# Second feed-forward entry: 1/z by ScalarE, squares added by DMAs, two more weights split in attention

## The chip, the cores and the metric

One core of a Trainium2 chip runs the whole program. The metric is the device time of one execution in microseconds (us), lower is better. The engines that matter here are TensorE (PE, matrix products), VectorE (DVE, elementwise), ScalarE (ACT, functions from tables, copies), GpSimd (POOL, which here issues transfers and reduces over partitions) and SyncE (SP, which only issues transfers). Each engine runs its own instructions in the order in which they were written and waits at an instruction until its inputs are there and its buffer is free.

## What is computed

Two layers of a decoder on a sequence of 1024 positions with 1024 channels: a short gated convolution, a dilated attention of three branches, and behind each of them a SwiGLU feed-forward network of 2816 hidden channels. Cut to what the change touches:

```
def rms_norm(x, g):
    y = xf * lax.rsqrt(jnp.mean(xf * xf, axis=-1, keepdims=True) + EPS)
    return (y * g).astype(x.dtype)

def dilated_attention_mixer(h, w_qkv, w_out, rel_bias):
    ...
    alpha = jax.nn.softmax(jnp.stack(lses, axis=0), axis=0)
    o = jnp.sum(alpha[..., None] * jnp.stack(outs, axis=0), axis=0)
    return o.reshape(bsz, seq, D_MODEL).astype(h.dtype) @ w_out

def reference(x, ...):
    for i in range(DEPTH):
        h = rms_norm(x, mix_norm[i])
        x = x + (short_conv_mixer(...) if i % 2 == 0 else dilated_attention_mixer(...))
        h = rms_norm(x, ffn_norm[i])
        x = x + swiglu(h, ffn_w_gate[i], ffn_w_up[i], ffn_w_down[i])
    return rms_norm(x, final_norm)
```

In the kernel the three branches of attention share one sum: `o` holds the unnormalised output of a pair of heads and `z` its denominators, so that the output is o times 1/z.

## The kernel before

Activations lie transposed: eight tiles X[0] to X[7] of 128 channels by 1024 positions, each worked on in two halves of 512 positions. Every float32 operand is split into a high and a low part of the type fp32r (`split`, L138 on ScalarE copies the high part, L139 on VectorE subtracts for the low part), and a product is three matmuls: high by high, high by low, low by high. Weights come from HBM through pages called `raw` (SP's queue, L152), are split, and stand in a list `ops` in the order of use; `ensure(n)` splits ahead up to place n of that list.

The place of the change is the end of attention and the entry into the second feed-forward network.

- **The last slot of attention.** The output product of attention has two groups: group 0 takes five of the eight head pairs, group 1 (`("ao", 1, n)`, weights of 128x384) takes pairs 5, 6 and 7. Group 0 runs inside the last slots as filling for TensorE. Just before the last slot, `ensure(ahead_ao)` splits the weights of group 1 for the first five tiles (`AO_WIDE` = 5).
- **`finish(p)`, last pair.** z and o are copied out of PSUM by ScalarE (L1486, L1487). For earlier pairs 1/z takes a way through DRAM. For the last pair VectorE takes the reciprocal of 128x256 pieces in place (L1518), multiplies o (L1512), and after each half o is split into `o_hi` and `o_lo`.
- **Group 1 (`by_columns`).** It runs the eight tiles of X for the first half and then for the second half, nine matmuls each (L347 to L349). The first three tiles of the first half run abreast. Behind each tile VectorE adds the product to X (L466), ScalarE squares the tile for the norm (`Norm.chained`) and sends it to a spill buffer (L1220), and some weights of the feed-forward network are split.
- **`Norm.chained`, the sum of squares.** In the second entry `by_dma` is false: the square of tile 0 goes to `acc` (L427), each later one to a buffer `sq` (L420) that VectorE adds to `acc` one tile later (L422). In the first entry `by_dma` is true: tile 1's square goes to a second buffer `acc2` (called `odd`); the squares of tiles 2 and 4 are added to `acc`, those of 3 and 5 to `acc2`, by transfers that accumulate, issued by POOL (L429); VectorE adds tile 6's square, `acc2` and tile 7's square (L430).
- **The statistics.** `stats` sums `acc` over channels on TensorE (L445), takes the root on ScalarE (L448) and the reciprocal on VectorE (L449), and spreads 1/rms over partitions by a diagonal matrix (L454) and a matmul (L461); ScalarE copies it to `rstd` (L462). For the first half this stands among the tiles of the second half. From then on VectorE makes the operands of the first half, `hcol` (L1063) and its low part (L526), between the additions to X. For the second half L445 stands behind the first two products of the feed-forward network (L533 to L535), and `second_half` (L1093) needs its `rstd`.
- `gained` (L1085, and L1089 by POOL's accumulating transfers) prepares the second half's operands.

PSUM has eight banks of 128x512, given out in turn; a bank is free again when the addition or copy that reads it is done. Nothing but the order in the code places the work.

Of the kernel before, what the change touches and what calls it, by code (L numbers as in the profile page):

```python
# [12 lines left out]
AF = mybir.ActivationFunctionType  # L13
ALU = mybir.AluOpType
# [3 lines left out]
S = 1024  # L18
# [5 lines left out]
HALF = 512  # L24
# [21 lines left out]
AO_WIDE = 5  # L46
# [48 lines left out]
def trunk(ctx: ExitStack, tc: tile.TileContext, x, gains_in, cwi, ck, cwo, wqkv, wo, relb,  # L95
          wg, wu, wd, oneh, ident, out):
    nc = tc.nc
# [6 lines left out]
    def page(name, dt=F32):  # L104
        return pages.tile([128, 1024], dt, name=name, tag="page", bufs=PAGES)
# [3 lines left out]
    def half_page(name, dt=F32):  # L109
        return scope["pool"].tile([128, 512], dt, name=name, tag="half", bufs=scope["halves"])  # L110
# [4 lines left out]
    def half(h):  # L115
        return slice(h * HALF, (h + 1) * HALF)
# [11 lines left out]
    def split(src, dst=None, eng=nc.vector):  # L128

        w = src.shape[1]  # L130
        if dst is None:
            if w <= HALF:
                t = page("w", F32R)
                dst = t[:, :w], t[:, HALF:HALF + w]
            else:
                dst = page("w_hi", F32R)[:, :w], page("w_lo", F32R)[:, :w]
        hi, lo = dst
        nc.scalar.activation(hi, src, AF.Copy)  # L138
        eng.tensor_tensor(out=lo, in0=src, in1=hi, op=ALU.subtract)  # L139
        return hi, lo  # L140
# [4 lines left out]
    ops, made, op_state = [], {}, [0, 0]  # L145
    combos, raw_base, sums_of = {}, {}, {}

    def load_raw(upto):
        while raw_state[0] < min(upto + 1, len(raw_src)):
            i = raw_state[0]  # L150
            raw_tile[i] = page("raw")
            nc.sync.dma_start(raw_tile[i][:, :raw_src[i].shape[1]], raw_src[i])  # L152
            raw_state[0] += 1
# [5 lines left out]
    def ensure(upto):  # L159
        while op_state[0] < min(upto + 1, len(ops)):  # L160
            key = ops[op_state[0] + 1][0] if op_state[0] + 1 < len(ops) else None
            if key in sums_of:
                sums_of.pop(key)()
            made[op_state[0]] = ops[op_state[0]][1]()
            op_state[0] += 1
# [186 lines left out]
    def run(*gens):  # L352
        for _ in zip(*gens):
            pass
        for g in gens:
            for _ in g:
                pass
# [12 lines left out]
    X = [None] * KT  # L370

    class Norm:
        def __init__(self, gi):
            self.g = gi
            self.h = {}
            self.acc = self.rstd = None
            self.put_off = None
            self.by_dma = True

        def flush(self):  # L380

# [22 lines left out]
        def add(self, k):  # L404

            hi, lo = page("h_hi", F32R), page("h_lo", F32R)
            nc.scalar.activation(hi, X[k], AF.Identity, scale=self.gain(k))
            nc.vector.scalar_tensor_tensor(lo, X[k], self.gain(k), hi, op0=ALU.mult, op1=ALU.subtract)
            self.h[k] = (hi, lo)
            self.square(k)  # L410

        def chained(self, k, c0, c1):

            s = slice(c0, c1)
            if self.acc is None:
                self.acc, self.rstd = page("acc"), page("rstd")
            acc = self.acc[:, s]
            if not self.by_dma and k:
                to = half_page("sq")
                nc.scalar.activation(to, X[k][:, s], AF.Square)  # L420
                self.flush()
                self.put_off = lambda: nc.vector.tensor_tensor(out=acc, in0=acc, in1=to, op=ALU.add)  # L422
                return
            if k == 1:
                self.odd = half_page("acc2")
            to = half_page("sq") if k > 1 else self.odd if k else acc
            nc.scalar.activation(to, X[k][:, s], AF.Square)  # L427
            if 1 < k < 6:
                nc.gpsimd.dma_start(out=(acc, self.odd)[k % 2], in_=to, accum_op=ALU.add)  # L429
            add = lambda t: nc.vector.tensor_tensor(out=acc, in0=acc, in1=t, op=ALU.add)  # L430
            if k == KT - 1:
                self.flush()
                add(self.odd)
                self.odd = None
            if k > 5:
                self.put_off = lambda: add(to)
# [615 lines left out]
    class Swiglu(Strassen):  # L1052
# [6 lines left out]
        def scaled(self, n, h, t, x=None):  # L1059

            rstd = self.norm.rstd[:, half(h)]
            if x is None:
                nc.vector.scalar_tensor_tensor(t, X[n][:, half(h)], self.norm.gain(n), rstd, op0=ALU.mult, op1=ALU.mult)  # L1063
            else:
                nc.vector.tensor_tensor(out=t, in0=x, in1=rstd, op=ALU.mult)
            return t
# [129 lines left out]
    def into_ffn(i, norm):  # L1196

        sw = Swiglu(i, norm)
        norm.by_dma = not i
        begin = i  # L1200

        pre = []
        first_op = [k for k, f in ops].index(("m", (i, 0), 1))

        def step(k):
            next(pre[0], None)
            sw.gained(k)

        def group1(key, ks, acts):
            def added(j, n):  # L1210

                if j == 0 and n > 3:
                    if n + 2 < KT:
                        ensure(op_state[1] + 1)
                    ensure(first_op + n - 4)
                elif j and n < 2:
                    ensure(first_op + n + 4)

            def between(j, n):
                nc.scalar.dma_start(spill[n][:, half(j)], X[n][:, half(j)])  # L1220
                if j == 0:
                    if n == 3:
                        load_raw(raw_base[i] + 3)
                        if not i:
                            nc.scalar.activation(less, gains, AF.Copy, scale=-1.0)
                    elif n == KT - 1:
                        norm.flush()
                        if i:
                            nc.scalar.activation(scratch, eps, AF.Sqrt)
                elif n == begin:  # L1230
                    pre.append(norm.stats(0, HALF))
                    next(pre[0])
                    for m in (6, 7):
                        combos[i, 0](m)
                elif n > begin:
                    if n == begin + 1:
                        run(pre.pop())
                        pre.append(sw.first_half())
                    plan = ((0, 1), (2,), (3,), (4,), (5,), (6, 7)) if i else ((0,), (1,), (2, 3), (4,), (5,), (6,), (7,))
                    for k in plan[n - begin - 1]:  # L1240
                        step(k)

            by_columns((key, 1), ks, acts, HALVES, lambda n, c: norm.chained(n, *c), between,
                       3 if key == "ao" else 4, added=added)

        def last_step():
            run(pre[0])
            norm.flush()

        return sw, group1, norm.stats(HALF, S), last_step  # L1250
# [19 lines left out]
    def attention(norm):  # L1270
# [11 lines left out]
        parts = {}  # L1282
# [207 lines left out]
        def finish(p):  # L1490

            o, z = OZ.pop(p)
            if p < NPAIR - 1:
                zd, rd = zdram[p]
                nc.sync.dma_start(zd, z[0:65:64])
                yield
                zc = scope["pool"].tile([128, 16], F32, name="zc", tag="zc", bufs=2)
                nc.sync.dma_start(zc, bass.AP(zd.tensor, zd.offset, [[16, 128], [1, 16]]))
                yield
                nc.vector.reciprocal(zc, zc)  # L1500
                nc.sync.dma_start(bass.AP(rd.tensor, rd.offset, [[16, 128], [1, 16]]), zc)
                yield
                nc.sync.dma_start(z, bass.AP(rd.tensor, rd.offset, [[S, 2], [0, 64], [1, S]]))
                yield
                put_off.append((p, o, z))
                return

            acts[p] = page("o_hi", F32R), page("o_lo", F32R)

            def scaled(c0, c1):  # L1510
                q = slice(c0, c1)
                nc.vector.tensor_tensor(out=o[:, q], in0=o[:, q], in1=z[:, q], op=ALU.mult)  # L1512

            def parts(h):
                split(o[:, half(h)], [t[:, half(h)] for t in acts[p]])

            for c in range(0, S, 256):
                nc.vector.reciprocal(z[:, c:c + 256], z[:, c:c + 256])  # L1518
                scaled(c, c + 256)
                if c % HALF:  # L1520
                    parts(c // HALF)
                yield

        def attended():
# [96 lines left out]
            next(later, None)  # L1621
        run(later)
        live = {}
        ahead_ao = [k for k, f in ops].index(("ao", 1, AO_WIDE - 1))
        for p in range(NPAIR):
            last = p == NPAIR - 1
            if p < NPAIR - 2:
# [58 lines left out]
    with tc.tile_pool(name="first", bufs=1) as scope["pool"]:  # L1686
# [4 lines left out]
        norm = Norm(1)  # L1691
# [11 lines left out]
    with tc.tile_pool(name="third", bufs=1) as scope["pool"]:  # L1703
# [3 lines left out]
        norm = Norm(4)  # L1707
# [135 lines left out]
```

## Time and profile before

| What | us |
|---|---|
| median of 3 runs | 2198.8 (2198.76 to 2199.12) |
| time of the profiled execution | 2194.63 |
| its span, first to last instruction | 2192.6 |
| mean granted clock of TensorE | 0.992 |
| ScalarE busy | 999.8 |
| GpSimd busy | 161.9 |

In the profile's rows a group or an instruction reads: line, engine, operation, output<-input by the program's names, shape, count; then busy time and the mean in ns of one, and the engine's idle time ahead with what ended it. In rows in order of time the start and the duration stand in front. An arrow in square brackets names the engine and tile that an instruction had waited for. Rows of stretches give the busy time and count of each engine, then the granted clock, the busy share of the transfer engines and GB/s.

### The profile page before, as it was taken

The page shows a single profiled execution, that of the slowest core. Times are in us where ns is not written, and L with a number is a line of the kernel's source. Part 1 is how long each engine was busy: PE and PEld are TensorE (multiplying, and loading weights), DVE is VectorE, ACT ScalarE, POOL GpSimd, SP SyncE. Part 2 cuts the span into 40 slices and gives each one's busy share as a digit, 9 for nine tenths or more (in the row PEclk, how much of TensorE's full clock was granted, in tenths as well). Part 3 has the DMA queues.
Part 4 walks back from the last instruction along what each step waited for, and adds up shares of the span by engine and source line. Part 5 has one row for each costly group of instructions (what it writes and reads, how often), then busy time and mean ns, then how long its engine had stood idle before and what let it go on. Part 6 is the DMA issues. An engine that isn't in the chain of part 4 may idle for free.

```text
span 2192.6 us, 30554 instructions
## 1 busy us (share of the span) xinstructions
PE 2133.3 (97%) x11138; PEld 1821.9 (83%) x11138; DVE 1759.4 (80%) x3239; ACT 999.8 (46%) x1812; POOL 161.9 (7%) x212
## 2 busy tenths in 40 slices
PE   7899999999999999999999999999999999999998
PEld 6788888778888878878999999887778888888887
DVE  7797848988888798965677777769988888889886
ACT  6433426444443444434455555525544444454435
POOL 0000001010101000010111111110000101000000
PEclk9999999999999999999999999999999999999999
DMA  4122543222323374423333333544223333365432
GB/s 155 54 83 75 204 156 92 97 92 97 120 97 120 93 280 144 132 82 132 91 91 91 91 91 84 170 124 165 71 77 106 108 103 107 100 234 194 159 91 78
DMA packets 133568, 259.50 MB, mean 118 GB/s; under 512 B 47642, under 2 KB 58922, under 8 KB 133418
## 3 DMA queue, kind: packets, MB, share of 16 engines
q1 hardware_dynamic: 75978, 184.80, 26.1%
q0 software_dynamic: 16272, 49.65, 6.4%
q10 hardware_dynamic: 41168, 23.10, 3.5%
q8 instruction: 88, 1.44, 0.3%
q14 instruction: 62, 0.51, 0.1%
HBM read 187.04 MB, written 66.26 MB: 116 GB/s over the span
## 4 chain that ended last, share of the span: by engine, by line
PE 78%; DVE 13%; ACT 4%; DMA 3%; issue 2%; ACTq 0%; SPq 0%; DVEq 0%
PE bank L533 15%; PE bank L535 15%; PE bank L534 15%; PE bank L349 5%; PE bank L347 5%; PE bank L348 5%; PE bank L1463 4%; PE bank L625 3%; PE bank L627 3%; PE bank L628 3%; DVE w L139 2%; DVE b L526 1%; DVE combo L186 1%; PE bank L1391 1%; PE bank L1390 1%
## 5 line engine op out<-in xcount | busy, mean ns | idle before, releaser
L533 PE MATMUL bank<-b,w 128*128 128x512 f32 x1784 | 704.6, 395 | 25.7 <-DVE part L543 6.4
L535 PE MATMUL bank<-b,w 128*128 128x512 f32 x1784 | 700.7, 393 | 8.7 <-DVE w L139 8.7
L534 PE MATMUL bank<-b,w 128*128 128x512 f32 x1784 | 701.2, 393 | 0.0
L533 PEld LDWEIGHTS bank<-b,w 128*128 128x128 f32 x1784 | 338.8, 190 | 102.1 <-ACT part L539 7.5
L535 PEld LDWEIGHTS bank<-b,w 128*128 128x128 f32 x1784 | 338.7, 190 | 84.1 <-DVE w L139 12.7
L534 PEld LDWEIGHTS bank<-b,w 128*128 128x128 f32 x1784 | 338.5, 190 | 69.7 <-issue 0.7
L138 ACT ACTIVATE w<-combo 128x512 fp32r<-128x512 f32 (+2 forms) x464 | 234.5, 534 | 281.2 <-DVE combo L186 275.2
L139 DVE TENSOR_TENSOR w<-combo,w 128x512 fp32r<-128x512 f32 (+2 forms) x464 | 260.2, 574 | 57.6 <-ACT w L138 56.0
L539 ACT ACTIVATE part<-bank 128x512 f32<-128x512 f32 x168 | 99.5, 593 | 270.2 <-PE bank L535 265.1
L139 DVE TENSOR_TENSOR w<-raw,w 128x512 fp32r<-128x512 f32 (+2 forms) x316 | 169.1, 559 | 17.2 <-ACT w L138 15.6
L543 DVE TENSOR_TENSOR part<-part,bank 128x256 f32<-128x256 f32 (+1 forms) x348 | 158.5, 485 | 26.5 <-PE bank L535 14.3
L138 ACT ACTIVATE w<-raw 128x512 fp32r<-128x512 f32 (+2 forms) x316 | 150.6, 519 | 46.4 <-PE bank L535 11.2
L754 DVE TENSOR_TENSOR x<-x,bank 128x512 f32<-128x512 f32 x168 | 114.2, 680 | 31.1 <-PE bank L535 31.0
L347 PE MATMUL bank<-w_hi,w 128*128 128x512 f32 (+1 forms) x320 | 119.8, 374 | 2.6 <-ACT w L138 2.6
L349 PE MATMUL bank<-w_hi,w 128*128 128x512 f32 (+1 forms) x320 | 118.1, 369 | 0.7 <-DVE w L139 0.7
L348 PE MATMUL bank<-w_lo,w 128*128 128x512 f32 (+1 forms) x320 | 117.8, 368 | 0.0
L466 DVE TENSOR_TENSOR x<-x,bank 128x512 f32<-128x512 f32 (+1 forms) x104 | 66.0, 641 | 60.5 <-PE bank L349 52.2
L186 DVE TENSOR_TENSOR combo<-raw 128x512 f32<-128x512 f32 (+1 forms) x160 | 102.9, 643 | 3.8 <-DMA raw<-in_conv_w_in 3.8
L347 PE MATMUL bank<-h_hi,w_hi 128*128 128x512 f32 x256 | 104.6, 409 | 0.0
L349 PE MATMUL bank<-h_hi,w_lo 128*128 128x512 f32 x256 | 100.2, 391 | 0.7 <-DVE w_lo L139 0.7
L348 PE MATMUL bank<-h_lo,w_hi 128*128 128x512 f32 x256 | 99.9, 390 | 0.0
L1137 ACT ACTIVATE part<-part 128x512 f32<-128x512 f32 x66 | 39.7, 628 | 109.7 <-DVE part L543 109.7
(249 smaller groups left out, 3835.2 us busy)
## 6 DMA issues: line engine op xcount, KB each, us to landing
hin<-part SPq DMA_DIRECT2D x126, 256.0 KB
raw<-in_ffn_w_gate SPq DMA_DIRECT2D x44, 512.0 KB
raw<-in_ffn_w_up SPq DMA_DIRECT2D x44, 512.0 KB
part<-sum POOLq DMA_DIRECT2D x72, 256.0 KB, 2.7
raw<-in_ffn_w_down SPq DMA_DIRECT2D x48, 384.0 KB
x<-spill SPq DMA_DIRECT2D x24, 512.0 KB
raw<-in_attn_w_qkv SPq DMA_DIRECT2D x24, 512.0 KB
raw<-in_conv_w_in SPq DMA_DIRECT2D x21, 512.0 KB
```

Source lines behind the costliest of these rows:

```text
L138: nc.scalar.activation(hi, src, AF.Copy)
L139: eng.tensor_tensor(out=lo, in0=src, in1=hi, op=ALU.subtract)
L186: eng.tensor_tensor(out=c, in0=a, in1=b, op=op)
L347: nc.tensor.matmul(b, whi[:, a], ahi[:, s], start=first, stop=False)
L348: nc.tensor.matmul(b, whi[:, a], alo[:, s], start=False, stop=False)
L349: nc.tensor.matmul(b, wlo[:, a], ahi[:, s], start=False, stop=last)
L533: nc.tensor.matmul(b, hi[:, a], bhi, start=start and k == 0, stop=False, skip_group_check=True)
L534: nc.tensor.matmul(b, hi[:, a], blo, start=False, stop=False, skip_group_check=True)
L535: nc.tensor.matmul(b, lo[:, a], bhi, start=False, stop=k == n - 1, skip_group_check=True)
L539: nc.scalar.activation(t, b, AF.Copy)
L543: nc.vector.tensor_tensor(out=t, in0=t, in1=b, op=ALU.add)
L754: nc.vector.tensor_tensor(out=X[n][:, half(h)], in0=X[n][:, half(h)], in1=b, op=ALU.add)
```

## The change

Three edits.

1. For the last pair, 1/z is exp(-ln z): ScalarE takes Ln of the whole z (128x1024) and then, by halves, Exp with scale -1; VectorE multiplies a half of o at a time. The reciprocals are gone.
2. `by_dma` is gone: the second entry adds the squares of tiles 2 to 5 by transfers, as the first does.
3. `ahead_ao` reaches two weights further: seven of group 1's eight weights are split before the last slot.

```diff
-            self.by_dma = True
...
-            if not self.by_dma and k:
-                to = half_page("sq")
-                nc.scalar.activation(to, X[k][:, s], AF.Square)
-                self.flush()
-                self.put_off = lambda: nc.vector.tensor_tensor(out=acc, in0=acc, in1=to, op=ALU.add)
-                return
...
-        norm.by_dma = not i
...
-            for c in range(0, S, 256):
-                nc.vector.reciprocal(z[:, c:c + 256], z[:, c:c + 256])
-                scaled(c, c + 256)
-                if c % HALF:
-                    parts(c // HALF)
+            nc.scalar.activation(z, z, AF.Ln)
+            for h in range(2):
+                nc.scalar.activation(z[:, half(h)], z[:, half(h)], AF.Exp, scale=-1.0)
+                scaled(h * HALF, h * HALF + HALF)
+                parts(h)
                 yield
...
-        ahead_ao = [k for k, f in ops].index(("ao", 1, AO_WIDE - 1))
+        ahead_ao = [k for k, f in ops].index(("ao", 1, AO_WIDE + 1))
```

Line numbers of the changed kernel are 7 or 8 lower than those of the kernel before (L466 is L459, L422 is gone, L430 is L423, L526 is L519, L1063 is L1056).

How the order moves, first on ScalarE at the end of the last slot, from the splits of group 1's weights to the first square. Before:

```order
L138 ACTIVATE w<-raw 128x384 x5
L1486 ACTIVATE z<-bank 64x512
L1487 ACTIVATE o<-bank 64x512
L1486 ACTIVATE z<-bank 64x512
L1487 ACTIVATE o<-bank 64x512
L138 ACTIVATE o_hi<-o 128x512 x2
L427 ACTIVATE acc<-x 128x512
```

And with the change:

```order
L138 ACTIVATE w<-raw 128x384 x7
L1478 ACTIVATE z<-bank 64x512
L1479 ACTIVATE o<-bank 64x512
L1478 ACTIVATE z<-bank 64x512
L1479 ACTIVATE o<-bank 64x512
L1509 ACT_TABLE_LOAD
L1509 ACTIVATE z<-z 128x1024
L1511 ACT_TABLE_LOAD
L1511 ACTIVATE z<-z 128x512
L138 ACTIVATE o_hi<-o 128x512
L1511 ACTIVATE z<-z 128x512
L138 ACTIVATE o_hi<-o 128x512
```

Two splits stand ahead of the copies of z, and two table loads, one Ln and two Exp between the copies and `o_hi`.

On VectorE, the end of the second half's stretch, from the addition to tile 6 of X to the last addition of squares. Before:

```order
L466 TENSOR_TENSOR x<-x,bank 128x512
L422 TENSOR_TENSOR acc<-acc,sq 128x512
L1063 SCALAR_TENSOR_TENSOR hcol<-x,gains,rstd 128x512
L526 TENSOR_TENSOR b<-hcol,b 128x512
L466 TENSOR_TENSOR x<-x,bank 128x512
L422 TENSOR_TENSOR acc<-acc,sq 128x512
L1063 SCALAR_TENSOR_TENSOR hcol<-x,gains,rstd 128x512
L526 TENSOR_TENSOR b<-hcol,b 128x512
L1063 SCALAR_TENSOR_TENSOR hcol<-x,gains,rstd 128x512
L526 TENSOR_TENSOR b<-hcol,b 128x512 x2
L422 TENSOR_TENSOR acc<-acc,sq 128x512
```

And with the change:

```order
L459 TENSOR_TENSOR x<-x,bank 128x512
L1056 SCALAR_TENSOR_TENSOR hcol<-x,gains,rstd 128x512
L519 TENSOR_TENSOR b<-hcol,b 128x512
L459 TENSOR_TENSOR x<-x,bank 128x512
L423 TENSOR_TENSOR acc<-acc,sq 128x512
L423 TENSOR_TENSOR acc<-acc,acc_13620 128x512
L1056 SCALAR_TENSOR_TENSOR hcol<-x,gains,rstd 128x512
L519 TENSOR_TENSOR b<-hcol,b 128x512
L1056 SCALAR_TENSOR_TENSOR hcol<-x,gains,rstd 128x512
L519 TENSOR_TENSOR b<-hcol,b 128x512 x2
L423 TENSOR_TENSOR acc<-acc,sq 128x512
```

The additions of squares between the tiles are gone; behind tile 7 stand those of tile 6's square, of the second buffer (`acc_13620`, the `acc2` of the code) and, last as before, of tile 7's square.

On POOL, from the last transfer of attention to the second half's transfers (L1082 is L1089 before). Before, the four `x<-x` followed the first row at once; with the change:

```order
L1521 DMA odram_91<-o 128x1024
L422 DMA acc<-sq 128x512
L422 DMA acc_13482<-sq 128x512
L422 DMA acc<-sq 128x512
L422 DMA acc_13482<-sq 128x512
L422 DMA acc<-sq 128x512
L422 DMA acc_13620<-sq 128x512
L422 DMA acc<-sq 128x512
L422 DMA acc_13620<-sq 128x512
L1082 DMA x<-x 128x512 x4
```

Eight accumulating transfers have come in, four for each half, two and two into one buffer.

## The prediction

> **What bounds the kernel now.** I read the page's first part, then the waits of TensorE and its order of time around the entry into the second feed-forward network, then what VectorE and ScalarE do there.
>
> ```profile
> span 2192.6 us, 30554 instructions
> PE 2133.3 (97%) x11138; PEld 1821.9 (83%) x11138; DVE 1759.4 (80%) x3239; ACT 999.8 (46%) x1812; POOL 161.9 (7%) x212
> ```
>
> TensorE sets the time: only its waits can be won. The profiled execution took 2194.63 us (span 2192.6); the median of the runs is 2198.8, 4.2 above. The sums below are made in the span, and I take their difference off the median. The waits of TensorE from 1483 to 1600 us, where all three edits lie (total, times, longest):
>
> ```profile
> PE bank L445 <- DVE acc L422: 4.0, 1, 4.0
> PE bank L535 <- DVE w L139: 2.3, 2, 1.9
> PE bank L347 <- ACT w L138: 1.6, 1, 1.6
> ```
>
> In order of time, with the last matmul before each wait and the first ones after it:
>
> ```profile
> 1500.60 0.39 PE L349 MATMUL bank<-o_hi,w 128*128 128x512 f32 x1
> 1502.57 0.50 PE L347 MATMUL bank<-w_hi,w 128*128 128x512 f32 x1 [1.58 <-ACT w L138]
> ...
> 1532.75 0.39 PE L535 MATMUL bank<-b,w 128*128 128x512 f32 x1
> 1537.16 1.05 PE L445 MATMUL bank<-ones,acc 128*128 128x1 f32 x8 [4.02 <-DVE acc L422]
> 1538.07 0.60 PE L533 MATMUL bank<-b,w 128*128 128x512 f32 x1
> ...
> 1541.81 0.39 PE L533 MATMUL bank<-b,w 128*128 128x512 f32 x1
> ```
>
> At full clock a matmul of 512 columns starts every 0.23 us. **Loss A**: 1502.57 - 1500.60 - 0.23 = 1.74 us, for the sixth output weight. **Loss B**: 1537.16 - 1532.75 - 0.23 = 4.18 us, for the sum of squares of the second half. **Loss C**: behind B the nine matmuls from 1538.07 take 3.74 us where 9 x 0.23 = 2.07 would do: 1.7 us, at half clock. Together 7.6 us, the most that this change can win. The 2.3 us at L535 lie after the second statistics, and no edit touches them.
>
> Why VectorE is late, by its groups from 1485 to 1538:
>
> ```profile
> L466 DVE TENSOR_TENSOR x<-x,bank 128x512 f32<-128x512 f32 x19 | 12.7, 679 | 0.0
> L422 DVE TENSOR_TENSOR acc<-acc,sq 128x512 f32<-128x512 f32 x14 | 9.6, 685 | 0.3
> L1518 DVE RECIPROCAL z<-z 128x256 f32<-128x256 f32 x4 | 7.0, 1745 | 0.0
> ```
>
> Its idle time there is about 3 us of 53: it runs behind TensorE throughout, and the four reciprocals put it there. Neighbours overlap, so that an addition of 128x512 costs 0.60 us from start to start.
>
> **The change part by part.** *Two more weights split in attention.* Tile 5 of the product finds its weight; tile 6 likewise, and tile 7's is split after tile 3's square, some 4 us before use. Loss A goes: -1.74. The price is two splits ahead of the copies of z on ScalarE.
>
> *1/z by ScalarE.* VectorE loses 7.0 us of reciprocals; its four multiplications become two of twice the width. ScalarE gains two table loads, Ln and two Exp; their prices, and the landing of a weight from SP's queue:
>
> ```profile
> 1481.31 2.16 ACT L138 ACTIVATE w<-raw 128x384 fp32r<-128x384 f32 x5
> 1485.33 0.59 ACT L1487 ACTIVATE o<-bank 64x512 f32<-64x512 f32 x1
> 1510.08 0.64 ACT L420 ACTIVATE sq<-x 128x512 f32<-128x512 f32 x1 [0.65 <-DVE x L466]
> 1510.73 1.28 ACT L1229 ACT_TABLE_LOAD   x1
> L1453 ACT ACTIVATE lf<-lf 128x1024 f32<-128x1024 f32 x16 | 16.9, 1056 | 45.1 <-DMA vx<-vdram 24.2 <-DVE lf L1452 20.8
> ...
> 1481.97 0.33 SPq L152 DMA_DIRECT2D raw<-in_attn_w_out  x1
> 1494.93 0.39 PE L348 MATMUL bank<-o_lo,w 128*128 128x512 f32 x1
> ...
> 1459.97 0.32 SPq L1607 DMA_DIRECT2D x<-spill  x1
> 1462.73 0.69 DVE L466 TENSOR_TENSOR x<-x,bank 128x512 f32<-128x512 f32 x1 [7.85 <-DMA x<-spill]
> 1475.77 0.32 SPq L1597 DMA_DIRECT2D oin<-odram  x1
> 1480.35 1.06 ACT L138 ACTIVATE w_hi<-oin 128x1024 fp32r<-128x1024 f32 x1 [0.95 <-DMA oin<-odram]
> ```
>
> The seventh weight is issued at 1481.97. Two loads of this queue took 2.8 and 4.6 us until their reader ran; I take 2.8, the emptier queue: split 1484.8 to 1485.2, four copies to 1487.7 (1485.9 before). Then 1.28 + 1.06 (Exp's row for Ln) + 1.28 + 0.63 = 4.25: 1491.9. Multiplication, o_hi, o_lo at some 0.7 each: 1494.0. TensorE wants o_lo at 1494.93: 0.9 to spare, so it costs nothing; the cover is the two other tiles of the product ahead. With 4.6 us it would be 0.9 late, and all behind it too. VectorE waits meanwhile with two additions to tile 7 of x behind it; their banks come back five tiles later. From 1499 it has caught up with TensorE.
>
> *Squares by DMA.* Of seven additions per half three stay. Where the first half's sum ends, VectorE is no longer late. The stretch that sets B:
>
> ```profile
> 1513.39 0.68 DVE L466 TENSOR_TENSOR x<-x,bank 128x512 f32<-128x512 f32 x1
> ...
> 1518.12 0.68 DVE L466 TENSOR_TENSOR x<-x,bank 128x512 f32<-128x512 f32 x1
> 1519.99 1.41 DVE L1063 SCALAR_TENSOR_TENSOR hcol<-x,gains,rstd 128x512 f32<-128x512 f32 x2 [1.19 <-ACT rstd L462]
> ...
> 1522.05 0.68 DVE L466 TENSOR_TENSOR x<-x,bank 128x512 f32<-128x512 f32 x1
> 1522.64 0.69 DVE L422 TENSOR_TENSOR acc<-acc,sq 128x512 f32<-128x512 f32 x1
> 1523.24 0.74 DVE L1063 SCALAR_TENSOR_TENSOR hcol<-x,gains,rstd 128x512 f32<-128x512 f32 x1
> ...
> 1536.42 0.68 DVE L422 TENSOR_TENSOR acc<-acc,sq 128x512 f32<-128x512 f32 x1
> ```
>
> The addition at 1513.39 (tile 1, second half) now follows its bank, which A's end brings to 1511.5; its square, r and diag (0.6 to 1.0 us each) reach 1514.1, three combos 1516.0, tile 2's addition and square 1517.3, rstd 1517.9. So hcol starts at 1517.9, not 1519.99: 2.1 us earlier. From there to TensorE's L445 it was 17.17 us of queued VectorE work; five additions of squares leave it and two come in: 17.17 - 3 x 0.60 = 15.4. The sum is ready for TensorE at 1533.3; I add 0.1 for a landing (below): 1533.4 against 1537.16, a gain of **3.7**. TensorE comes there at 1532.98 - 1.74 = 1531.2, so a wait of 2.2 stays in place of 4.18: A's 1.74 + 2.0 is the same 3.7. All behind, rstd and the second half's operands, moves with it.
>
> The eight DMAs run as in the first entry. L1089's four stand behind them on POOL, an engine that is 7% busy:
>
> ```profile
> PE bank L445 <- DVE acc L430: 0.8, 1, 0.8
> ...
> DMA to landing us min/median/max: 3.2/3.2/4.2
> ...
> DMA to landing us min/median/max: 3.2/3.4/5.1
> ```
>
> These are TensorE's wait for the sums there, the landing of its eight accumulating DMAs, and of the eight of L1089 (same size, same queue, four of them in this entry). Tiles 3 and 5 add into one buffer, one after the other; tile 5's square ends at 1525.0, and VectorE wants the sum at 1528.7: 3.7 us. At 3.2 no wait, at 4.2 one of 0.5, at 5.1 of 1.4; 0.1 taken.
>
> **Loss C** depends on the clock. Two other waits and the granted clock (last column but two) in the 3 us behind these and behind A:
>
> ```profile
> 71.56 0.47 PE L533 MATMUL bank<-b,w 128*128 128x512 f32 x1 [2.17 <-DVE part L543]
> 71.60:74.60 3.00, 3.00 (x13) 2.38 (x14) 2.79 (x5) 1.90 (x4) 0.00 (x0) 1.00 0.39 85
> 1640.43 0.60 PE L533 MATMUL bank<-b,w 128*128 128x512 f32 x1 [2.25 <-ACT part L539]
> 1640.50:1643.50 3.00, 3.00 (x8) 2.35 (x9) 2.31 (x7) 1.71 (x6) 0.00 (x0) 0.53 0.00 0
> 1502.60:1505.60 3.00, 3.00 (x13) 2.30 (x14) 3.00 (x6) 2.31 (x5) 0.00 (x0) 1.00 1.02 301
> ```
>
> A wait of 1.58 leaves the clock whole; 2.25 halves it, 2.17 does not. A wait of 2.2 may go either way; I let the half clock stay, so C gives nothing. The Trainium skill (TensorE: Matmul & The Clock Gate, "HAM oscillation — how this bites in real kernels") says that gaps over about 3.4 us throttle; by it C would go, as in the first rival, but the wait of 2.25 speaks against it.
>
> Sum: 2198.8 - 3.7 = **2195.1 us**. Its own range: rstd 0.5 earlier or 0.3 later, landings up to 5.1: gain 2.2 to 4.4, 2194.4 to 2196.6.
>
> **Rivals.** *The half clock goes too.* The 2.2 us of wait do not halve the clock: gain 3.7 + 1.7 = 5.4, 2193.4. For it the row at 71.56, against it that at 1640.43.
>
> *Wait B goes wholly.* If VectorE gets 2.2 us ahead of my sum, all 7.6 us are won: 2191.2. For it the first entry, where the second half's sum costs TensorE nothing; against it that a tile of this product has 9 matmuls, 2.1 us, in which VectorE has 1.9 us of its own.
>
> *1/z comes late.* Table loads or the seventh weight take longer than my rows, o_lo passes 1494.93, and every us beyond is lost on TensorE: 0.9 late by the 4.6 us landing, 2196.0. Against it: the row at 1510.73 starts 0.01 us after the square before it ends, with no pause. The Trainium skill (ScalarE: Activation LUTs, "What ACT_TABLE_LOAD costs") adds a drain of 1.38 us to each switch; two would make o_lo 1.9 late, 2197.0 by an estimate from that page; the trace's row shows none.
>
> *The accumulating DMAs are the new wait: slower.* VectorE stands in order at the sum of the two buffers, and rstd, hcol and all operands behind it. Tile 3's DMA starts at 1521.4 and tile 5's cannot start before it lands: ready at 1521.4 + 2 landings. Above 3.7 us each further us costs two; at 5.5 the whole gain is gone, at 7.7 the kernel is 4.4 slower: 2203.2. For it: 5.1 us among L1089's landings, with spills and weight loads in the same 16 engines; against it the first entry's 4.2 at most.
>
> **How the numbers follow.** Forecast 0.43, half clock gone 0.25, wait gone 0.10, 1/z late 0.12, DMAs late 0.10. 0.2% is 4.4 us, about what a measurement tells from none. Faster by more: the first two rivals and a fifth of the forecast, 0.44. Slower by more: most of the last, 0.08. Within: 0.48. The range reaches from the whole 7.6 us and a little to a gain wholly lost: 2190.8 to 2199.8.
>
> **What would show it.** Right: no wait at the sixth output weight; Exp's last half and o_lo before TensorE's o_lo matmul; VectorE idle behind banks between 1499 and 1511; a wait of about 2 us at the second L445, some 3.7 us earlier; eight landings near 3.2. Wrong: a wait at the o_hi matmuls, VectorE idle at the sum of the two buffers, or a second L445 later than 1535.

## The result: 0.19% slower, and the profile after

The changed kernel takes 2201.43 us (median of 20 runs, 2199.43 to 2205.13) where the kernel before takes 2197.76 on the same chip (20 runs, 2194.50 to 2199.34): a ratio of 1.0019 (of the means; the medians are 3.7 us apart), 95% interval 1.0012 to 1.0026, or 4.2 us of 2198 (2.6 to 5.7). 2195.1 was forecast. The profiled executions differ by more, 2201.0 against 2192.6 us of span: that of the kernel before is 3.1 us quicker than its median, that of the changed kernel 1.3 slower. The page of the changed kernel, first part:

```profile
span 2201.0 us, 30553 instructions
PE 2136.7 (97%) x11138; PEld 1824.9 (83%) x11138; DVE 1749.7 (79%) x3225; ACT 1005.5 (46%) x1817; POOL 168.2 (8%) x220
```

VectorE has 9.7 us less work, as meant, and the kernel is slower all the same. TensorE's waits of the changed kernel from 1483 to 1620 us (total, times, longest). What were L445 and L535 are now L438 and L528:

```profile
PE bank L438 <- DVE acc L423: 8.8, 2, 5.6
PE bank L528 <- DVE w L139: 2.5, 2, 1.9
```

The wait at the sixth output weight is gone. The wait for the sum of squares was one of 4.0 us and is now two, 8.8 us together. Where they lie, on TensorE in order of time:

```profile
1497.59 0.39 PE L348 MATMUL bank<-o_lo,w 128*128 128x512 f32 x1
...
1513.45 0.39 PE L349 MATMUL bank<-o_hi,w 128*128 128x512 f32 x1
1519.42 1.86 PE L438 MATMUL bank<-ones,acc 128*128 128x1 f32 x8 [5.58 <-DVE acc L423]
1521.15 0.77 PE L347 MATMUL bank<-w_hi,w 128*128 128x512 f32 x1
...
1545.81 1.05 PE L438 MATMUL bank<-ones,acc 128*128 128x1 f32 x8 [3.22 <-DVE acc L423]
```

And two rows of TensorE of the kernel before, the first half's sum and the next small wait behind the second half's:

```profile
1513.03 0.94 PE L445 MATMUL bank<-ones,acc 128*128 128x1 f32 x8
...
1569.20 0.50 PE L535 MATMUL bank<-b,w 128*128 128x512 f32 x1 [0.43 <-DVE w L139]
```

The first matmul with o_lo stands at 1497.59, before at 1494.93: 2.66 us were lost ahead of the change, 2.49 of them by 1062 us, in code that it does not touch. Executions differ so: in the experiments below this matmul stands between 1494.23 and 1498.19. To compare profiles I count from this matmul. The first half's sum comes 21.83 us behind it (18.10 before, without a wait), the second half's 48.22 (42.23 before): 6.0 us later. VectorE of the changed kernel at these places:

```profile
1496.07 0.69 DVE L139 TENSOR_TENSOR o_lo<-o,o_hi 128x512 fp32r<-128x512 f32 x1 [0.70 <-ACT o_hi L138]
...
1498.67 3.67 DVE L459 TENSOR_TENSOR x<-x,bank 128x512 f32<-128x512 f32 x6
...
1515.81 0.69 DVE L423 TENSOR_TENSOR acc<-acc,sq 128x512 f32<-128x512 f32 x1 [4.72 <-DMA acc<-sq]
1517.88 0.69 DVE L423 TENSOR_TENSOR acc<-acc,acc 128x512 f32<-128x512 f32 x1 [1.38 <-DMA acc<-sq]
...
1527.59 1.42 DVE L1056 SCALAR_TENSOR_TENSOR hcol<-x,gains,rstd 128x512 f32<-128x512 f32 x2 [1.53 <-ACT rstd L455]
...
1541.15 0.69 DVE L423 TENSOR_TENSOR acc<-acc,acc 128x512 f32<-128x512 f32 x1 [2.67 <-DMA acc<-sq]
```

In the first half VectorE stands idle for 4.72 + 1.38 us before additions whose other operand a DMA has still to add to; in the second half for 2.67 us. hcol starts 30.00 us behind the first o_lo matmul, 25.06 before. The accumulating DMAs of the changed kernel on GpSimd, and their landings (minimum, median, maximum) for the first two, the next two and the four of the second half:

```profile
1502.72 1.77 POOL L422 DMA_DIRECT2D acc<-sq  x2 [26.66 <-DMA spill<-x]
1511.07 0.84 POOL L422 DMA_DIRECT2D acc<-sq  x1 [6.59 <-issue]
1514.59 0.84 POOL L422 DMA_DIRECT2D acc<-sq  x1 [2.68 <-issue]
```

```profile
DMA to landing us min/median/max: 7.8/8.6/9.4
...
DMA to landing us min/median/max: 3.2/4.0/4.7
...
DMA to landing us min/median/max: 3.2/4.0/5.3
```

Tiles 2 and 3 took 7.8 and 9.4 us instead of 3.2; tile 4's DMA adds into the same buffer as tile 2's, so it was issued at 1511.07, and tile 5's at 1514.59. Two stretches of the changed kernel (busy times, then granted clock, share of the transfer engines, GB/s):

```profile
1518.00:1520.00 2.00, 0.58 (x3) 0.58 (x3) 1.90 (x4) 0.00 (x1) 0.00 (x0) 0.50 0.00 0
...
1502.00:1504.00 2.00, 2.00 (x11) 1.65 (x10) 0.67 (x2) 1.95 (x4) 1.28 (x2) 1.00 1.04 395
```

When the first two DMAs are issued, the 16 transfer engines are full at 395 GB/s; when the wait ends, the clock is at 0.50. What else was in flight: spills issued from 1500.59 on, and two weight loads of 512 KB by SP at 1502.80, which had been held for 11.4 us by the landing of a spill (SP's issues and its waits in the changed kernel):

```profile
1502.80 0.83 SPq L152 DMA_DIRECT2D raw<-in_ffn_w_up  x2
```

```profile
SPq L152 <- DMA spill<-x: 11.4, 1, 11.4
```

### The profile page after: what moved, and what is told of

It reads as the page before. It is cut to its first block, busy times and chain, and to the rows that moved or that the text cites. A ratio compares the mean times of both kernels' runs of the same rounds, so it can differ in the third digit from the quotient of the medians.

```text
span 2201.0 us, 30553 instructions
## 1 busy us (share of the span) xinstructions
PE 2136.7 (97%) x11138; PEld 1824.9 (83%) x11138; DVE 1749.7 (79%) x3225; ACT 1005.5 (46%) x1817; POOL 168.2 (8%) x220
## 4 chain that ended last, share of the span: by engine, by line
PE 79%; DVE 10%; ACT 4%; DMA 3%; issue 3%; ACTq 0%; POOL 0%; SPq 0%; DVEq 0%; POOLq 0%
PE bank L526 16%; PE bank L528 16%; PE bank L527 16%; PE bank L349 5%; PE bank L347 5%; PE bank L348 5%; PE bank L1455 4%; PE bank L620 3%; PE bank L621 3%; PE bank L618 3%; DVE w L139 2%; PE bank L1383 1%; PE bank L1382 1%; DVE combo L186 1%; DVE b L519 1%
## 5 line engine op out<-in xcount | busy, mean ns | idle before, releaser
L526 PE MATMUL bank<-b,w 128*128 128x512 f32 x1784 | 705.1, 395 | 27.1 <-DVE part L536 6.4
L528 PE MATMUL bank<-b,w 128*128 128x512 f32 x1784 | 701.2, 393 | 9.5 <-DVE w L139 9.5
L526 PEld LDWEIGHTS bank<-b,w 128*128 128x128 f32 x1784 | 339.0, 190 | 103.3 <-ACT part L532 8.1
L528 PEld LDWEIGHTS bank<-b,w 128*128 128x128 f32 x1784 | 338.7, 190 | 85.3 <-DVE w L139 14.0
L459 DVE TENSOR_TENSOR x<-x,bank 128x512 f32<-128x512 f32 (+1 forms) x104 | 65.8, 643 | 63.9 <-PE bank L349 55.6
```

The source lines that it names most:

```text
L526: nc.tensor.matmul(b, hi[:, a], bhi, start=start and k == 0, stop=False, skip_group_check=True)
L528: nc.tensor.matmul(b, lo[:, a], bhi, start=False, stop=k == n - 1, skip_group_check=True)
```

## The experiments

Ratios are to the kernel before, with 95% intervals, those of the experiments from 9 to 11 runs each; 0.001 is 2.2 us. "First sum", "hcol" and "second sum" are us behind the first o_lo matmul in the profiled execution.

```
kernel                               ratio   interval           first sum  hcol   second sum
before                               1                          18.10      25.06  42.23
changed: all three parts             1.0019  1.0012 to 1.0026   21.83      30.00  48.22
e1  1/z and splits, no DMAs          0.9987  0.9978 to 0.9996   16.10      22.90  40.08
e2  DMAs alone                       1.0021  1.0012 to 1.0031   21.64      29.15  48.08
e3  1/z alone                        0.9986  0.9977 to 0.9995   16.35      23.30  40.47
e4  splits alone                     0.9990  0.9981 to 0.9998   16.50      24.39  41.57
e5  all, DMAs in second half only    0.9998  0.9989 to 1.0007   16.25      23.09  42.32
e6  all, DMAs in first half only     1.0018  1.0008 to 1.0027   21.75      29.41  46.59
c1  all, spills four tiles later     1.0004  0.9995 to 1.0013   17.97      25.96  44.26
c4  all, two weight loads sooner     1.0003  0.9994 to 1.0012   17.90      25.25  44.42
e7  e1, DMAs for two late tiles      0.9988  0.9979 to 0.9997   16.10      22.59  39.29
e8  e1, four late squares on GpSimd  0.9991  0.9982 to 1.0000   16.09      22.59  40.81
```

### Which part loses

**e1**, the changed kernel without its DMAs.

```diff
+            self.by_dma = True
...
+            if not self.by_dma and k:
+                to = half_page("sq")
+                nc.scalar.activation(to, X[k][:, s], AF.Square)
+                self.flush()
+                self.put_off = lambda: nc.vector.tensor_tensor(out=acc, in0=acc, in1=to, op=ALU.add)
+                return
...
+        norm.by_dma = not i
```

> The change without its second part: 1/z by ScalarE and the two more splits stay, all squares are added by VectorE as before. Theory T (the accumulating DMAs land late, 7.8 and 9.4 us in the first half, and are the whole loss; the other two parts gain what was forecast): no wait of TensorE at the sixth output weight, none at the first half's sum, the second half's sum at most 2.1 us earlier than before, in all 2 to 4 us faster than before (2194 to 2196 where before has 2197.8). Rival R1 (1/z by ScalarE or the splits delay the entry, and the DMAs only show it): slower than before by 2 us or more, with a wait at the first half's sum as in the changed kernel.

Measured: ratio 0.9987, 2194.92 us. TensorE and VectorE of e1:

```profile
1498.19 0.39 PE L348 MATMUL bank<-o_lo,w 128*128 128x512 f32 x1
...
1514.29 0.95 PE L445 MATMUL bank<-ones,acc 128*128 128x1 f32 x8
...
1538.27 1.86 PE L445 MATMUL bank<-ones,acc 128*128 128x1 f32 x8 [4.01 <-DVE acc L422]
...
1571.34 0.50 PE L535 MATMUL bank<-b,w 128*128 128x512 f32 x1 [0.56 <-DVE w L139]
```

```profile
1521.09 1.42 DVE L1063 SCALAR_TENSOR_TENSOR hcol<-x,gains,rstd 128x512 f32<-128x512 f32 x2 [1.19 <-ACT rstd L462]
```

No wait at the sixth weight, none at the first half's sum; hcol starts 2.16 us earlier than before, and from it to the second sum are 17.18 us (17.17 before). Parts one and three gain; the loss is the DMAs'.

**e2**, the kernel before with the DMAs alone.

```diff
-            if not self.by_dma and k:
+            if not self.by_dma and k and not (True):
```

> The kernel before with the second part alone: the squares of tiles 2 to 5 added by DMAs in the second entry too; the reciprocals stay on VectorE and the splits where they were. Theory T: the landings are late here too, since spills and weight loads are in flight at the same place; a wait of 3 to 6 us at the first half's sum, 2 to 6 us slower than before (2200 to 2204). Rival R1: same as before or faster, landings of 3 to 5 us. Rival R2 (the DMAs are late only because ScalarE and VectorE, rid of the reciprocals, do tiles 0 to 4 in a bunch): landings near 4 us, no wait at the first half's sum, 0 to 3 us faster than before.

Measured: ratio 1.0021, landings of the first three DMAs of 5.8 to 8.7 us, a wait of 4.64 us at the first half's sum:

```profile
1518.05 1.87 PE L445 MATMUL bank<-ones,acc 128*128 128x1 f32 x8 [4.64 <-DVE acc L430]
```

```profile
DMA to landing us min/median/max: 5.8/6.4/8.7
```

So the DMAs lose as much without the other two parts, and the bunching of tiles behind a quicker 1/z is not needed for it. **e5** and **e6** have all parts, but DMAs in one half only. Against e1:

```diff
-            if not self.by_dma and k:
+            if not self.by_dma and k and not (c0 >= HALF):
```

That is e5; in e6 the last condition is `c0 < HALF`.

> The changed kernel with VectorE adding the squares in the first half, DMAs in the second half alone. Theory T, with all of the loss in the first half: no wait at the first half's sum, hcol some 5 us earlier than in the changed kernel, the second half's landings 3 to 5 us; 3 to 4.5 us faster than before (2193.5 to 2195). If the second half's landings cost too: the wait at the sum of the two buffers stays near 2.7 us, and the kernel is within 1.5 us of before. Rival R1: slower than before by 2 us or more.

> The changed kernel with DMAs in the first half alone, VectorE adding the squares of the second. Theory T: landings of 7 to 10 us, the wait of 5.6 us at the first half's sum and the half clock behind it stay, and the second half's sum comes as late as in the changed kernel or later; 3 to 7 us slower than before (2201 to 2205). Rival (the second half's DMAs are the loss): within 1.5 us of before.

Measured: e5 0.9998, e6 1.0018. Against e1 the first half's DMAs cost 6.5 us at the second sum (46.59 against 40.08), the second half's 2.2 (42.32). My first case for e5, that all of the loss lies in the first half, was wrong; the second, that landings there cost too, held. In e6 the second sum comes 1.6 us sooner than in the changed kernel; as late or later was expected. The two accumulating DMAs of e5 that share `acc2` (tiles 3 and 5), on GpSimd, and VectorE, which waits for the second:

```profile
1524.46 0.86 POOL L429 DMA_DIRECT2D acc<-sq  x1 [3.32 <-ACT sq L427]
...
1530.18 0.84 POOL L429 DMA_DIRECT2D acc<-sq  x1 [3.22 <-ACT b L525]
```

```profile
1530.60 0.69 DVE L430 TENSOR_TENSOR acc<-acc,sq 128x512 f32<-128x512 f32 x1
1535.04 0.69 DVE L430 TENSOR_TENSOR acc<-acc,acc 128x512 f32<-128x512 f32 x1 [3.74 <-DMA acc<-sq]
```

VectorE is ready at 1531.30. From tile 3's issue to the sum it is 10.58 us, 5.3 for each of the two turns, though the landings themselves measure 3.8 and 4.8: tile 5's DMA is issued 1.9 us after tile 3's landed. What these 1.9 us are was not settled; in the changed kernel the same gap is 0.5 us (1535.77 less 1531.58 and a landing of 3.7), and the two turns there take 9.57 (to 1541.15). In e6 the landing view of the first two DMAs reads:

```profile
DMA to landing us min/median/max: 8.2/8.8/9.4
```

### Why the first two land late

**c1**, the changed kernel with the first half's spills four tiles later.

```diff
-                nc.scalar.dma_start(spill[n][:, half(j)], X[n][:, half(j)])
+                keep = lambda t, g: nc.scalar.dma_start(spill[t][:, half(g)], X[t][:, half(g)])
+                if i:
+                    if n > 3 - 4 * j and n < 8 - 4 * j:
+                        keep(n - 4 + 8 * j, 0)
+                    if j:
+                        keep(n, 1)
+                else:
+                    keep(n, j)
```

> The changed kernel, with the copies of x's first half to the spill (256 KB each, on ScalarE's queue) issued four tiles later, so that four of them no longer stand in the transfer engines when the first two accumulating DMAs are issued. Theory S (the spills and the two weight loads ahead of them hold the accumulating DMAs up): landings of the first two fall from 7.8 and 9.4 us to 5 or less, the wait at the first half's sum from 5.6 to 2.5 or less, its half clock goes; the second half, with twice the spills, may lose 1 to 2 us; in all 2 to 6 us faster than the changed kernel (2196 to 2200). Rival W (the two weight loads of 512 KB, or the software queue itself, hold them up): landings of 7 us or more stay, the wait stays over 4 us, the same time as the changed kernel or slower.

Measured: ratio 1.0004, 3.3 us better than the changed kernel (0.0015). SP's weight loads, the landings of the first three DMAs, and the first half's sum, of c1:

```profile
1492.29 5.44 SPq L152 DMA_DIRECT2D raw<-in_ffn_w_up  x2
```

```profile
DMA to landing us min/median/max: 3.2/3.6/4.8
```

```profile
1515.74 1.67 PE L438 MATMUL bank<-ones,acc 128*128 128x1 f32 x8 [1.72 <-DVE acc L423]
```

The landings are short again and the wait with them, but the half clock behind it, which was expected to go, stays (last section). And with the spills the two weight loads had moved as well, ten microseconds sooner, since no spill held them any more. So c1 shows that other transfers in flight are the cause, and not which. **c4** moves the loads alone.

```diff
             def between(j, n):
+                if i and j == n == 0:
+                    load_raw(raw_base[i] + 5)
                 nc.scalar.dma_start(spill[n][:, half(j)], X[n][:, half(j)])
```

> The changed kernel, with the two up-weight loads of 512 KB issued some 10 us sooner, ahead of the first spill, while the spills stay where they were. In the run with later spills these loads had moved too, since each load takes turns with an earlier spill; this run separates the two. Theory L (the two loads, issued 0.1 us behind the first accumulating DMA, hold it up): landings of the first two fall from 7.8 and 9.4 us to 5.5 or less, the wait at the first half's sum from 5.6 to 3 or less, 2 to 5 us faster than the changed kernel (2196.5 to 2199.5). Theory S (the four spills of 256 KB ahead of them suffice): landings of 7 us or more, the wait over 4 us, within 1.5 us of the changed kernel (2200 to 2203). Between the two: landings of 5.5 to 7, a wait of 3 to 4.5.

Measured: ratio 1.0003. Loads, third spill, landings of the first three DMAs and the first half's sum, of c4:

```profile
1492.03 1.91 SPq L152 DMA_DIRECT2D raw<-in_ffn_w_up  x2
```

```profile
1502.36 0.42 ACTq L1214 DMA_DIRECT2D spill<-x  x1
```

```profile
DMA to landing us min/median/max: 3.3/3.7/5.0
```

```profile
1516.03 1.30 PE L438 MATMUL bank<-ones,acc 128*128 128x1 f32 x8 [1.65 <-DVE acc L423]
```

The spills stand where they stood, 1.0 MB of them within 2 us, and the landings are 3.3 to 5.0 us. So the two loads, 512 KB each, issued together with the first accumulating DMA, are needed for the 7.8 and 9.4; whether they would do it without the spills beside them was not run. The transfer engines are as full in c4 as in the changed kernel (share 1.04, the last column but one):

```profile
1504.00:1508.00 4.00, 4.00 (x19) 3.31 (x18) 3.05 (x5) 2.64 (x5) 1.88 (x3) 1.00 1.04 253
```

Without the loads the wait at the first half's sum is 1.65 us instead of 5.58. That is still no gain: two landings of some 4 us one after the other remain, and the second half's wait with them.

### What the two good parts are worth, and whether more can be had

**e3** is the kernel before with part one alone, **e4** with part three alone.

```diff
-            for c in range(0, S, 256):
-                nc.vector.reciprocal(z[:, c:c + 256], z[:, c:c + 256])
...
+            nc.scalar.activation(z, z, AF.Ln)
+            for h in range(2):
+                nc.scalar.activation(z[:, half(h)], z[:, half(h)], AF.Exp, scale=-1.0)
...
```

```diff
-        ahead_ao = [k for k, f in ops].index(("ao", 1, AO_WIDE - 1))
+        ahead_ao = [k for k, f in ops].index(("ao", 1, AO_WIDE + 1))
```

> The kernel before with the first part alone: 1/z of the last pair by ScalarE. Measured from the first o_lo matmul, hcol's start came 25.06 us later before, and 22.90 with the first and third part together. Theory V (VectorE, late through its reciprocals, sets hcol; loss A then shifts all behind it): the wait at the sixth weight stays, hcol some 24 to 24.7, 0.4 to 1 us faster than before (2197 to 2198). Rival: it has the whole gain of the two (hcol at 22.9, 2 us faster or more). Rival: the Ln and two Exp delay the splits of output weights, the wait at the sixth grows past 3 us and the kernel is slower.

> The kernel before with the third part alone: two more output weights split in attention. Theory V: the wait at the sixth weight goes, but VectorE is still late through the reciprocals, so hcol stays within 0.7 us of its 25.06 behind the first o_lo matmul: same as before within 1 us. Rival: the 1.7 us of the wait are won to the end (hcol near 23.3, 1.7 us faster).

Measured: e3 0.9986, e4 0.9990. My theory for e3 was wrong: without any more splits the wait at the sixth weight is gone, and e3 has the gain of e1 within the intervals. ScalarE of the kernel before, and of e3, ahead of that weight (the fourth square, then the splits; the first o_lo matmul of e3 is at 1494.23):

```profile
1501.47 0.63 ACT L420 ACTIVATE sq<-x 128x512 f32<-128x512 f32 x1 [0.76 <-DVE x L466]
...
1502.01 1.86 ACT L138 ACTIVATE w<-raw 128x384 fp32r<-128x384 f32 x4
```

```profile
1499.00 0.63 ACT L420 ACTIVATE sq<-x 128x512 f32<-128x512 f32 x1 [0.17 <-DVE x L466]
...
1499.54 1.86 ACT L138 ACTIVATE w<-raw 128x384 fp32r<-128x384 f32 x4
```

The split stands behind the fourth square, the square behind VectorE's addition to X, and that behind the reciprocals: 7.08 us behind the first o_lo matmul before, 5.31 in e3. The wait at the weight was VectorE's lateness by another road. e4 meets its theory at hcol (24.39, 0.67 sooner); its time, 2.2 us faster with an interval of 0.4 to 4.2, is more than the 1 us that I allowed, though the interval still holds 1 us. The profile shows 0.66 us of it at the second sum; where the rest would lie it does not show.

**e7** and **e8** start from e1. e7 gives the squares of tiles 2 and 3 of the second half to DMAs, e8 those of tiles 2 to 5 to GpSimd's own additions; both go into tile 1's square, which VectorE adds at tile 7.

```diff
             if not self.by_dma and k:
-                to = half_page("sq")
+                late = c0 >= HALF
+                if late and k == 1:
+                    self.odd = half_page("acc2")
+                to = self.odd if late and k == 1 else half_page("sq")
                 nc.scalar.activation(to, X[k][:, s], AF.Square)
+                if late and k == 1:
+                    return
+                if late and k < 4:
+                    nc.gpsimd.dma_start(out=self.odd, in_=to, accum_op=ALU.add)
+                    return
                 self.flush()
+                if late and k == KT - 1:
+                    nc.vector.tensor_tensor(out=acc, in0=acc, in1=self.odd, op=ALU.add)
```

In e8 `k < 6` stands for `k < 4`, and `nc.gpsimd.tensor_tensor(out=self.odd, in0=self.odd, in1=to, op=ALU.add)` for the DMA.

> The first and third part, VectorE adds all squares but those of tiles 2 and 3 of the second half, which DMAs add into tile 1's square, one after the other. In the run with four such DMAs there, they were issued at 1520.3 and 1524.5, and VectorE would have wanted the second sum at 1531.3; now each has 7 us or more. Theory D (a DMA costs nothing while its issue lies two landings of 5 us ahead of its reader): no wait of VectorE at the sum of the two buffers, VectorE has two additions (1.2 us) less, the second sum is at TensorE 38.9 us behind the first o_lo matmul against 40.08 without DMAs; 1 to 1.5 us faster than that kernel (2193 to 2194 where before has 2198), more if the half clock behind the wait goes. Rival (the DMAs slow the squares, spills or copies around them): the same as that kernel or slower.

> The first and third part; the squares of tiles 2 to 5 of the second half are added into tile 1's square by GpSimd itself, VectorE adds all others. No addition of GpSimd is in the traces; its nearest row is a fill of 64x1024 at 0.95 us, so some 1 to 1.9 us each are taken, and the four squares come 1.9 us apart. Theory V (VectorE's queue between hcol and the second sum sets loss B, and what leaves it is won if it lands without transfer): three additions (1.8 us) less on VectorE, no wait at the sum of the two buffers, the second sum 38.3 us behind the first o_lo matmul (40.08 without, 42.32 with four DMAs there); 1.5 to 2.5 us faster than the kernel without DMAs (2193 where before has 2198). Rival (GpSimd's additions take over 3 us each, or slow VectorE's own while they run): the second sum at 40 us or later, the same as that kernel or slower.

Measured: e7 0.9988, e8 0.9991. In e7 VectorE does not wait for the DMAs and the second sum comes 0.8 us sooner than in e1, but the time shows no gain over e1; 0.8 us would be lost in the intervals. TensorE in e7:

```profile
1536.63 1.86 PE L456 MATMUL bank<-ones,acc 128*128 128x1 f32 x8 [3.52 <-DVE acc L433]
```

In e8 GpSimd's additions are short enough, 1.29 to 1.61 us, but VectorE's own instructions stretch beside them. GpSimd and VectorE in e8:

```profile
1525.66 1.38 POOL L427 TENSOR_TENSOR acc<-acc,sq 128x512 f32<-128x512 f32 x1 [0.33 <-ACT sq L423]
```

```profile
1519.52 2.07 DVE L1074 SCALAR_TENSOR_TENSOR hcol<-x,gains,rstd 128x512 f32<-128x512 f32 x2 [1.19 <-ACT rstd L473]
...
1525.81 1.78 DVE L537 TENSOR_TENSOR b<-hcol,b 128x512 fp32r<-128x512 f32 x1
```

The hcol pair takes 2.07 us (1.42 in e1) and one subtraction 1.78 (0.69 in other places). The three additions that left VectorE are eaten up: second sum at 40.81, not 38.3. So the rival held.

Faster than both kernels are e1, e3, e4, e7 and e8 (the interval of e8 reaches 1.0000). Their intervals do not tell them apart. e3 has the lowest median, 2194.24 us, with part one alone: 0.14% faster than before.

## Why the prediction was wrong

- **1/z by ScalarE** was right. The first half of o_lo was ready at 1496.76 (1496.07 + 0.69), which is 1494.10 on the time of before (less 2.66); 1494.0 was forecast, 1494.93 the deadline. The end fits, the way to it only in part: the seven splits did not wait for the seventh weight, as in the sum, but ran together from 1484.89, behind a transfer of `oin` that came 0.9 us later than before. No matmul with o_hi or o_lo waited, in the changed kernel or in e1 and e3.
- **hcol 2.1 us earlier** was right for parts one and three: 2.16 in e1. Of the forecast gain of 3.7 us this much is real; e1's ratio says 2.9 us (0.9 to 4.8).
- **Loss A** goes, but the step had the wrong owner: it falls to part one alone as well, and of its 1.58 us of wait 0.30 are left in e2, which touches neither 1/z nor the splits. So A and the lateness of VectorE were one loss.
- **The step that failed** is the one on the squares: "Where the first half's sum ends, VectorE is no longer late". That is true of VectorE's work and says nothing of the landings, for which the first half had no term at all; the 0.1 us for landings was worked out for the second half alone. Measured, the first half's DMAs cost 6.5 us at the second sum: hcol, forecast 2.1 us earlier, came 4.9 later in the changed kernel (30.00 against 25.06). I took landings of 3.2 to 4.2 us from the first entry. A row that I quoted for its clock showed full transfer engines at this place, 1.02 and 301 GB/s from 1502.60 to 1505.60 us; but that alone would not have given the term, for in the first entry they are as full (1.08 from 320 to 322 us) beside landings of 3.2 to 4.0, with four spills just ahead. What the first entry lacks at that point is the two loads from SP's queue, which the kernel before issues here at 1501.63. Nor did I use the 0.8 us in the first of the rows taken from there: that wait is the one at its first half's sum (331.59), though VectorE waits for no landing there.
- **15.4 us from hcol to the second sum** was wrong too: 19.23 in e5, against 17.18 with VectorE's additions. The 0.1 us counted one landing, from the end of tile 5's square; the fourth rival counted two, from tile 3's DMA, which at 5.1 us each is a wait of 2.9 and not of 1.4. This rival had the mechanism, the place and the price: two turns, one after the other, from tile 3's DMA, the whole gain gone at 5.5 us each. e5 has 5.3 each and a second sum 0.09 us behind that of before. I gave it 0.10, and only for the second half.
- **Loss C, the half clock,** stayed, as forecast, and came a second time behind the first half's sum. The forecast was for a wait of 2.2 us; those measured are 3.22 and 5.58, so it was not put to the test.
- A reading that nothing hangs on: VectorE's idle time from 1485 to 1538 is 4.1 us (48.9 busy), not about 3.

## What to carry to other kernels

Work moved from a busy engine to a transfer is paid in landing time, and the landing time is that of the place to which it moves: look at what else is issued there within a few microseconds, from which queue and how large, before taking a duration from another place. The share of the transfer engines alone did not tell the places apart here. Every reader on the way needs a term of its own, and two accumulations into one buffer make it two landings in a row. When an engine that runs late feeds several waits, undo the lateness first and count the waits again; parts that each cure the same wait do not add up.

## What the runs showed of the hardware

- The same 256 KB accumulating DMA landed in 3.2 us (least, in both entries), 3.3 to 5.0 beside four spills of 256 KB, and 5.8 to 9.4 when two loads of 512 KB from SP's queue were issued within a microsecond of it (changed kernel, e2, e6).
- A wait of 1.72 us before the first half's sum in c1 was followed by the half clock, while waits of 1.58 and 2.17 left it whole in the kernel before. The stretch behind it in c1:

```profile
1518.00:1520.00 2.00, 2.00 (x7) 1.52 (x6) 1.80 (x4) 0.60 (x2) 0.00 (x0) 0.50 0.92 355
```

- The same wait is followed by more or less of the half clock. Before and in e1 the second sum waits the same 4.0 us; its eight matmuls take 1.05 us in the one and 1.86 in the other, and to the next small wait it is 32.04 us (1569.20 - 1537.16) and 33.07 (1571.34 - 1538.27). What decides it was not tested. One microsecond of difference between two profiles of this kernel tells nothing for that reason. The Trainium skill (TensorE: Matmul & The Clock Gate, "HAM oscillation — how this bites in real kernels") warns of gaps over about 3.4 us; in c1 the half clock followed a gap of half that.
- VectorE's instructions with two inputs in SBUF took up to 2.6 times as long (1.78 against 0.69 us) while GpSimd added beside them. The Trainium skill (SBUF — State Buffer, "Who interferes with whom") says that a VectorE instruction with two SBUF inputs contends with a GpSimd instruction that reads SBUF, and calls the ports that they share an exclusive lock; the 1.78 us beside an addition of 1.38 agree with it.
